# Differential scores as rounded high/low products in place of a float32 product with a block-diagonal key

## The chip, the core and the metric

The kernel runs on one core of a Trainium2 chip. The metric is the device time of one execution in microseconds; lower is better. The engines that matter here are TensorE (PE: matrix products; PEld is its weight load), VectorE (DVE), ScalarE (ACT), GpSimd (POOL) and SyncE (SP, whose queue starts the loads). Each works through its own list of instructions in order and waits for the others by semaphores.

## The reference

Two transformer blocks on 256 tokens of width 1024: latent attention, a convolutional FFN, differential attention, a second FFN and a hybrid layer. The change lies in the differential attention. Each of 8 heads has two maps j of 64 dimensions; each map has scores with a distance penalty and a softmax of its own, and the second map is taken off the first:

```python
qkv = x @ w_qkv
q = qkv[..., :2 * H * d].reshape(b, s, H, 2, d)        # H = 8, d = 64
k = qkv[..., 2 * H * d:4 * H * d].reshape(b, s, H, 2, d)
v = qkv[..., 4 * H * d:].reshape(b, s, H, 2 * d)
sc = jnp.einsum('bqhjd,bkhjd->bhjqk', qb, k) * scale
sc = sc - slopes[None, :, None, None, None] * dist[None, None, None]
p = jax.nn.softmax(sc, -1)
a = p[:, :, 0] - lam * p[:, :, 1]
o = jnp.einsum('bhqk,bkhd->bqhd', a, v)
o = rms_norm(o, subln_g) * (1.0 - lam_init)
return o.reshape(b, s, H * 2 * d) @ w_o
```

## The kernel before

Products with weights are done in three rounded products (`mm3`, L131 to L133): both operands are split into a high part, rounded to the type float32r, and a low part, the rest; high times high, high times low and low times high are added. A weight chunk of 128x1024 comes into a raw buffer, ScalarE makes its high part (`wload`, L116) and VectorE its low part (L117).

The differential layer (`diff`) first makes v for all heads. Then it goes through the heads. For each, `wload` brings the weights of q and k, and 48 products of 256 columns give q and k of the head, transposed (128 dimensions on partitions, 256 tokens), in one bank `mm` of PSUM; there are two such banks. The first map holds partitions 0 to 63, the second 64 to 127. ScalarE copies q (L689) into `dq` and the first map's k (L691) into the block-diagonal key `kbd`; VectorE copies the second map's k (L692). `kbd` is 128 x (2 x 256), zero off its two blocks, so that one product of 512 columns gives the scores of both maps (L699), in plain float32, for each of two blocks of 128 query tokens. The distance penalty is added by a bfloat16 product into the same bank (L700).

There is one score bank `s` (the last block of the last head takes an `mm` bank). Behind the scores comes, for each block, `softmax_rows`: the maximum over keys (L379) and its scaling (L380) on VectorE, two exponentials with their sums on ScalarE (L383), the reciprocal of the sums (L385) on VectorE. Then VectorE scales by lambda (L703), scales the first map (L704) and adds the second (L705). TensorE transposes the result (L707), ScalarE copies it to `aT` (L708), and TensorE multiplies by v (L711). After heads 3 and 7 the four heads are normed: squares on ScalarE (L719), sums (L720), eleven small operations and the scaling (L725) on VectorE, transposes on TensorE (L173), and the split into high and low parts (L127 on ScalarE, L128 on VectorE). The product with w_o (`wide`) starts with the key tiles of heads 0 to 3 and ends with those of heads 4 to 7. `boundary` then begins the next norm; its first products on TensorE are those at L275.

A scheduler sets the order on every engine when the program is built: it takes the operations of the whole program and moves independent ones ahead, so that projections of the next heads, and later products with w_o, stand between the scores of one head. A change of a few operations can therefore move rows on all engines.

Of the kernel before, what the change touches and what calls it, by code (L numbers as in the profile page):

```python
# [9 lines left out]
F32 = mybir.dt.float32  # L10
# [27 lines left out]
def build(tc, a, out):  # L38
# [15 lines left out]
    def banks(c2, **tags):  # L54
        """four banks of a layer, by tag; the other four are accumulators"""
        assert sum(tags.values()) == 4
        uid[0] += 1
        psx[0] = c2.enter_context(tc.tile_pool(name=f"ps{uid[0]}", bufs=1, space=bass.MemoryType.PSUM, reuse_waits="tile"))
        psx[1] = tags
# [40 lines left out]
    tsl = [slice(0, P), slice(P, 2 * P)]  # L100

    def wload(src, n, part=1024, tag="w", hb=HB, pool=None, eng=None, mk=None, scale=None):
        """a weight chunk [128, n]; returns its parts as (high, low) float32r tiles"""
# [36 lines left out]
    def rsqrt(v, n, mul=1.0):  # L140
        """v [P, n] (all positive) -> mul/sqrt(v): bit guess, one tuned and one cubic step."""
# [21 lines left out]
        # y1 is -1/K1 of the first step's value  # L163
# [4 lines left out]
    def tposes(src_list, dst_hi, dst_lo=None, scale=None, eng="v", tag="sm"):  # L168
        """transpose [P,128] pieces into one bank, then move to dst ([P, n, 128] view)."""
# [17 lines left out]
    def behind(*ins):  # L187
        """what is traced here goes behind these instructions on their engines"""
# [13 lines left out]
    def newton(ss, n, width, ins=False, mid=None):  # L202
        """1/sqrt(mean(x^2)+eps) from the scaled sums of one or two parts: bit guess and two Newton
        steps, the first with tuned constants; the sums come scaled so that no factor is left over."""
# [27 lines left out]
    def postnorm(pool, tb, bnk, g_bc):  # L232
        """h += rmsnorm(y) g"""
# [13 lines left out]
    def postnorm_cut(pool, tb, cut, g_bc):  # L247
        """the same for the last token block, in pieces that go out as they are done"""
# [15 lines left out]
    def prenorm(tb, g_bc, aft, warm_):  # L264
        """xT = transpose(rmsnorm(h) g) as high and low parts; 1/rms enters through the transposing product"""
        ss = small(2, F32, "ss2")
        # without a gain here it is in the weights that follow
        hg = [xp.tile([P, 512], F32, tag=f"hg{tb}{f}", name=nm("hg"), bufs=1) if g_bc is not None else h[:, tb, hf[f]] for f in range(2)]
        for f in range(2):
            j_ = square(h[:, tb, hf[f]], D, ss, f)  # L270
            if warm_:
                # keeps the clock of the tensor engine up while it waits
                b_ = smb()
                for _ in range(3):
                    nc.tensor.matmul(b_, j_[:, :P], j_, start=True, stop=True)  # L275
# [31 lines left out]
    def boundary(accs, post, pre):  # L307
        """residual add of one sublayer and the norm of the next, a token block at a time;
        returns xT and what is left to do of it, by token block"""
# [34 lines left out]
    def wide(src4, xT, bnk, mk=None, eng=None, hold=(), k0=4, cut=False):  # L344
        """generator: bnk[tb][f] = x @ w, w [1024, 1024] in four chunks of two k tiles; a step is one k tile
        of one token block, the first block's before the second's"""
# [28 lines left out]
    # ================= layer 0: MLA =================  # L375
    def softmax_rows(e, s_ps, n_tb, scale, width=S):
        """s_ps [P, n, w] psum -> e = exp(scale*(s-max)), returns 1/sum [P, n]"""
# [10 lines left out]
    def mla(xT, fin):  # L388
        with ExitStack() as c2:
# [10 lines left out]
            # the first two k tiles as plain float32 products  # L400
# [57 lines left out]
            def v_of(tb):                         # tokens on partitions  # L458
# [9 lines left out]
            def qr_of(tb):                        # rope part of q  # L468
# [93 lines left out]
    # ================= conv FFN =================  # L562
    def ffn(li, xT, fin, pre):
        with ExitStack() as c2:
# [6 lines left out]
            # the first two column tiles as plain float32 products, each token block as it comes  # L571
# [67 lines left out]
    # ================= layer 1: differential attention =================  # L639
    def diff(xT, fin):  # L640
        with ExitStack() as c2:
# [13 lines left out]
            kbd = [lp.tile([P, 2, S], F32, tag=f"kbd{i}", name=f"kbd{i}") for i in range(2)]  # L655
            for t in kbd:
                nc.gpsimd.memset(t, 0.0)
            # v
# [23 lines left out]
            for hd in range(H):  # L682
# [5 lines left out]
                q = lp.tile([P, S], F32, tag="dq", name=nm("dq"), bufs=2)  # L688
                nc.scalar.copy(q, b[:, 0])  # L689
                kb = kbd[hd % 2]  # L690
                nc.scalar.copy(kb[0:64, 0], b[0:64, 1])  # L691
                nc.vector.tensor_copy(kb[64:128, 1], b[64:128, 1])  # L692
# [4 lines left out]
                for tb in range(2):  # L697
                    sb = (mmb() if hd == H - 1 and tb else bank("s")).rearrange("p (t s) -> p t s", t=2)
                    nc.tensor.matmul(sb, q[:, tsl[tb]], kb, start=True, stop=False)  # L699
                    nc.tensor.matmul(sb, sid[:, hd], distb[:, tb:tb + 1, :].to_broadcast([P, 2, S]), start=False, stop=True)  # L700
# [31 lines left out]
    # ================= hybrid layer =================  # L732
    def hybrid(xT, fin):
        with ExitStack() as c2:
# [48 lines left out]
            oball = Vik                           # o takes the place of v, tokens on partitions  # L783
# [63 lines left out]
            QK = lt("QK", [P, H, 2, S])   # [:, :, 0] = k', [:, :, 1] = q'  (both doubled)  # L847
# [65 lines left out]
            # M[i,j] = -(k_i.k_j) e^(G_i-G_j) c_j for j < i, stored with j on partitions (A) and with i on partitions (M)  # L913
# [47 lines left out]
            # (I - M)^-1 of the 16 x 16 diagonal blocks by substitution, one block on a partition  # L961
# [44 lines left out]
            # blocks of 16 -> 32 -> 64 -> 128; a pair's off-diagonal block lies in the even rows and odd columns  # L1006
# [36 lines left out]
            # outputs, four heads at a time  # L1043
# [44 lines left out]
            def zproj(br, hp):  # L1088
                """(1 + tanh(z/2)) z = 2 silu(z) of two heads"""
# [238 lines left out]
```

## Time and profile before

| what | value |
|---|---|
| median of three runs | 1039.8 us (1038.62 to 1041.2) |
| the profiled execution: span from first to last instruction | 1037.8 us |
| PE busy | 1012.7 us (98%) |
| DVE busy | 738.0 us (71%) |
| ACT busy | 545.3 us (53%) |
| POOL busy | 33.1 us (3%) |
| share of TensorE in the chain that ended last | 84% |

The page gives no other time for the profiled execution than its span. Matrix products are pipelined and their ends modelled, so one product's duration overlaps the next; what a product costs in a stream is the step from its start to the start of the next one. The same holds for VectorE and ScalarE, where a row can start a little before the one ahead has ended. The granted TensorE clock is full through the stretches of this layer.

### The profile page before, as it was taken

The page shows a single profiled execution, that of the slowest core. Times are in us where ns is not written, and L with a number is a line of the kernel's source. Part 1 is how long each engine was busy: PE and PEld are TensorE (multiplying, and loading weights), DVE is VectorE, ACT ScalarE, POOL GpSimd, SP SyncE. Part 2 cuts the span into 40 slices and gives each one's busy share as a digit, 9 for nine tenths or more (in the row PEclk, how much of TensorE's full clock was granted, in tenths as well). Part 3 has the DMA queues.
Part 4 walks back from the last instruction along what each step waited for, and adds up shares of the span by engine and source line. Part 5 has one row for each costly group of instructions (what it writes and reads, how often), then busy time and mean ns, then how long its engine had stood idle before and what let it go on. Part 6 is the DMA issues. An engine that isn't in the chain of part 4 may idle for free.

```text
span 1037.8 us, 18147 instructions
## 1 busy us (share of the span) xinstructions
PE 1012.7 (98%) x7120; PEld 924.6 (89%) x7120; DVE 738.0 (71%) x1387; ACT 545.3 (53%) x949; POOL 33.1 (3%) x35
## 2 busy tenths in 40 slices
PE   8889899999999999999999999999999999999997
PEld 6778799999987888799999998799898999999996
DVE  5775687777668479778777767578799657685563
ACT  5653466555436456557555554465554455544451
POOL 0000100000012000010000001000203000000000
PEclk9999999999999999999999999999999999999999
DMA  7562467555325425276655442444244413455541
GB/s 276 173 219 81 168 204 222 186 185 179 124 93 189 158 100 172 88 243 234 205 185 187 156 141 76 162 162 164 81 135 102 141 54 113 160 181 185 183 163 41
DMA packets 55301, 162.70 MB, mean 157 GB/s; under 512 B 12784, under 2 KB 15280, under 8 KB 55216
## 3 DMA queue, kind: packets, MB, share of 16 engines
q1 hardware_dynamic: 55216, 161.55, 47.4%
q8 instruction: 56, 0.92, 0.3%
q14 instruction: 29, 0.24, 0.1%
HBM read 160.08 MB, written 1.44 MB: 156 GB/s over the span
## 4 chain that ended last, share of the span: by engine, by line
PE 84%; DVE 9%; ACT 3%; DMA 2%; issue 1%; SPq 0%; POOL 0%; DVEq 0%; ACTq 0%; POOLq 0%
PE mm L131 11%; PE mm L132 11%; PE mm L133 11%; PE acc L132 8%; PE acc L131 8%; PE acc L133 8%; PE sm L133 4%; PE sm L132 4%; PE sm L131 4%; PE mm L583 2%; PE acc L1019 2%; DVE lo L117 1%; PE acc L1054 1%; PE s L699 1%; ACT junk L199 1%
## 5 line engine op out<-in xcount | busy, mean ns | idle before, releaser
L117 DVE TENSOR_TENSOR lo<-raw,hi 128x1024 fp32r<-128x1024 f32 (+1 forms) x271 | 326.5, 1208 | 140.6 <-ACT hi L116 139.4
L116 ACT CAST hi<-raw 128x1024 fp32r<-128x1024 f32 (+1 forms) x271 | 278.2, 1035 | 244.6 <-PE mm L132 126.6
L133 PE MATMUL mm<-xT,lo 128*128 128x256 f32 x928 | 265.6, 286 | 0.0
L131 PE MATMUL mm<-xT,hi 128*128 128x256 f32 x928 | 265.3, 286 | 0.0
L132 PE MATMUL mm<-xT,hi 128*128 128x256 f32 x928 | 264.9, 285 | 0.0
L132 PEld LDWEIGHTS mm<-xT,hi 128*128 128x128 f32 x928 | 177.6, 191 | 1.9 <-issue 0.7
L131 PEld LDWEIGHTS mm<-xT,hi 128*128 128x128 f32 x928 | 177.5, 191 | 1.5 <-issue 0.3
L133 PEld LDWEIGHTS mm<-xT,lo 128*128 128x128 f32 x928 | 177.6, 191 | 1.3 <-issue 0.7
L131 PE MATMUL sm<-xT,hi 128*128 128x256 f32 (+1 forms) x328 | 92.8, 283 | 0.0
L133 PE MATMUL sm<-xT,lo 128*128 128x256 f32 (+1 forms) x328 | 92.8, 283 | 0.0
L132 PE MATMUL sm<-xT,hi 128*128 128x256 f32 (+1 forms) x328 | 92.8, 283 | 0.0
L131 PE MATMUL acc<-hi,gv 128*128 128x512 f32 x176 | 69.2, 393 | 0.0
L132 PE MATMUL acc<-lo,gv 128*128 128x512 f32 x176 | 69.0, 392 | 0.0
L133 PE MATMUL acc<-hi,gv 128*128 128x512 f32 x176 | 68.5, 389 | 0.0
L132 PEld LDWEIGHTS sm<-xT,hi 128*128 128x128 f32 (+1 forms) x328 | 62.2, 190 | 0.9
L131 PEld LDWEIGHTS sm<-xT,hi 128*128 128x128 f32 (+1 forms) x328 | 62.2, 190 | 0.8
L133 PEld LDWEIGHTS sm<-xT,lo 128*128 128x128 f32 (+1 forms) x328 | 62.2, 190 | 0.1
L383 ACT ACTIVATE e<-s,s 128x256 f32<-128x256 f32 x46 | 21.5, 472 | 34.6 <-DVE s L380 32.8
L133 PEld LDWEIGHTS acc<-hi,gv 128*128 128x128 f32 x176 | 33.1, 188 | 7.5 <-DVE gv L125 0.3
L131 PEld LDWEIGHTS acc<-hi,gv 128*128 128x128 f32 x176 | 33.2, 189 | 6.3 <-ACT gv L125 0.6
L132 PEld LDWEIGHTS acc<-lo,gv 128*128 128x128 f32 x176 | 33.2, 189 | 5.3
L131 PE MATMUL mm<-og,hi 128*128 128x256 f32 x128 | 36.0, 281 | 0.0
(462 smaller groups left out, 1905.0 us busy)
## 6 DMA issues: line engine op xcount, KB each, us to landing
raw<-in_ffn_up SPq DMA_DIRECT2D x88, 512.0 KB, 4.6
raw<-in_ffn_down SPq DMA_DIRECT2D x44, 512.0 KB, 4.4
raw<-in_diff_qk SPq DMA_DIRECT2D x16, 512.0 KB, 5.2
raw<-in_h_kq SPq DMA_DIRECT2D x16, 512.0 KB, 4.5
raw<-in_h_qk SPq DMA_DIRECT2D x16, 512.0 KB, 3.9
raw<-in_h_z SPq DMA_DIRECT2D x16, 512.0 KB, 3.7
raw<-in_h_gate SPq DMA_DIRECT2D x16, 512.0 KB, 4.5
raw<-in_h_br SPq DMA_DIRECT2D x16, 512.0 KB, 4.6
```

The source lines that it names most:

```text
L116: nc.scalar.copy(hi[:, :k], raw[:, :k])
L117: (eng or nc.vector).tensor_tensor(lo[:, :k], raw[:, :k], hi.bitcast(F32)[:, :k], op=ALU.subtract)
L131: nc.tensor.matmul(o, l[0], r[0], start=start, stop=False)
L132: nc.tensor.matmul(o, l[0], r[1], start=False, stop=False)
L133: return nc.tensor.matmul(o, l[1], r[0], start=False, stop=stop)
L199: nc.scalar.activation(junk[:, :p.shape[-1]], p, AF.Square, scale=math.sqrt(beta_of(width)), accum_out=ss[:, i:i + 1])
L383: nc.scalar.activation(e[:, i], s_ps[:, i], AF.Exp, bias=mx[:, i:i + 1], scale=scale, accum_out=sm[:, i:i + 1])
L583: last = nc.tensor.matmul(mmf[j][:, t, tsl[tb]], raws[j][t][:, kt * P:kt * P + P], xF[kt // 4][:, kt % 4, tsl[tb]], start=kt == 0, stop=kt ...
L699: nc.tensor.matmul(sb, q[:, tsl[tb]], kb, start=True, stop=False)
L1019: nc.tensor.matmul(b[:, i], lhs(i), rhs(i), start=True, stop=True)
L1054: nc.tensor.matmul(b[:, i], lhs(hds[i], i), rhs(hds[i], i), start=True, stop=True)
```

## The change

For each head q and k are no longer copied as float32. Per map m there is a tile `qk[m]` of 128 x (2 x 256) in float32r. ScalarE casts the map's 64 rows of q and k into the map's own half of the partitions (L694). The other half gets the low part of q, which VectorE makes by a subtraction (L696), and once more the high part of k, which ScalarE copies (L697). So one product over 128 partitions adds high times high and low times high. `klo` holds the low part of k in the map's half, a second subtraction on VectorE (L698), and zeros in the other; the product with it adds high times low. A block's scores become one distance product and four products of 256 columns in place of one float32 product of 512 columns and one distance product. The distance product comes first.

The core of the diff:

```diff
-            kbd = [lp.tile([P, 2, S], F32, tag=f"kbd{i}", name=f"kbd{i}") for i in range(2)]
-            for t in kbd:
-                nc.gpsimd.memset(t, 0.0)
+            klo = [lp.tile([P, 2, S], F32R, tag=f"klo{i}", name=f"klo{i}") for i in range(2)]
+            for t in klo:
+                nc.gpsimd.memset(t.bitcast(F32), 0.0)
...
-                q = lp.tile([P, S], F32, tag="dq", name=nm("dq"), bufs=2)
-                nc.scalar.copy(q, b[:, 0])
-                kb = kbd[hd % 2]
-                nc.scalar.copy(kb[0:64, 0], b[0:64, 1])
-                nc.vector.tensor_copy(kb[64:128, 1], b[64:128, 1])
+                b2 = [slice(0, 64), slice(64, P)]
+                qk = [lp.tile([P, 2, S], F32R, tag=f"qk{m}", name=nm("qk"), bufs=2) for m in range(2)]
+                kl = klo[hd % 2]
+                for m in range(2):
+                    nc.scalar.copy(qk[m][b2[m]], b[b2[m]])
+                for m in range(2):
+                    nc.vector.tensor_tensor(qk[m][b2[1 - m], 0], b[b2[m], 0], qk[m].bitcast(F32)[b2[m], 0], op=ALU.subtract)
+                    nc.scalar.copy(qk[m][b2[1 - m], 1], qk[m].bitcast(F32)[b2[m], 1])
+                    nc.vector.tensor_tensor(kl[b2[m], m], b[b2[m], 1], qk[m].bitcast(F32)[b2[m], 1], op=ALU.subtract)
...
-                    nc.tensor.matmul(sb, q[:, tsl[tb]], kb, start=True, stop=False)
-                    nc.tensor.matmul(sb, sid[:, hd], distb[:, tb:tb + 1, :].to_broadcast([P, 2, S]), start=False, stop=True)
+                    nc.tensor.matmul(sb, sid[:, hd], distb[:, tb:tb + 1, :].to_broadcast([P, 2, S]), start=True, stop=False)
+                    for m in range(2):
+                        nc.tensor.matmul(sb[:, m], qk[m][:, 0, tsl[tb]], qk[m][:, 1], start=False, stop=False)
+                        nc.tensor.matmul(sb[:, m], qk[m][:, 0, tsl[tb]], kl[:, m], start=False, stop=m == 1)
```

Lines behind the change move down by eight: L703 to L705 become L711 to L713, L720 becomes L728, L725 becomes L733. Some comments and docstrings go as well, which changes nothing.

Outside this layer no engine's order changes. Inside it, three places. On TensorE, the scores of head 2's first block, before:

```order
L132 MATMUL mm_3969<-xT_3314,hi_3959 128x256
L699 MATMUL s_3918<-kbd_3418,dq_3912 128x512
L707 MATMUL sm_3811<-c_ident,e_3832 128x128 x2
L700 LDWEIGHTS sid
L700 MATMUL s_3918<-distb,sid 128x512
L133 MATMUL mm_3969<-xT_3313,lo_3960 128x256
```

and now (mm is a projection bank, hi and lo are weights, sid and distb the slope and the distances):

```order
L131 MATMUL mm_4005<-xT_3313,hi_3995 128x256
L705 LDWEIGHTS sid
L705 MATMUL s_3948<-distb,sid 128x512
L707 MATMUL s_3948<-qk_3936 128x256
L708 MATMUL s_3948<-klo_3418,qk_3936 128x256
L707 MATMUL s_3948<-qk_3937 128x256
L132 MATMUL mm_4005<-xT_3314,hi_3995 128x256
L708 MATMUL s_3948<-klo_3418,qk_3937 128x256
```

One row has become four, the distance product stands ahead of them, and a projection product fills in before the last.

On VectorE, head 1's second block and the preparation of head 2 before (s are the small columns of maxima and sums, e the softmax rows):

```order
L379 TENSOR_REDUCE s_3833<-s_3829 128x2
L380 TENSOR_SCALAR s_3833<-s_3833 128x2
L385 RECIPROCAL s_3839<-s_3836 128x2
L703 TENSOR_TENSOR s_3839<-s_3839,nlam 128x1
L704 TENSOR_SCALAR e_3832<-e_3832,s_3839 128x256
L692 COPY kbd_3418<-mm_3863 64x256
L705 SCALAR_TENSOR_TENSOR e_3832<-e_3832,s_3839 128x256
L117 TENSOR_TENSOR lo_4215<-raw_4212,hi_4214 128x1024
```

and now:

```order
L379 TENSOR_REDUCE s_3857<-s_3850 128x2
L117 TENSOR_TENSOR lo_4275<-raw_4272,hi_4274 128x1024
L380 TENSOR_SCALAR s_3857<-s_3857 128x2
L696 TENSOR_TENSOR qk_3936<-mm_3887,qk_3936 64x256
L698 TENSOR_TENSOR klo_3418<-mm_3887,qk_3936 64x256
L696 TENSOR_TENSOR qk_3937<-mm_3887,qk_3937 64x256
L385 RECIPROCAL s_3863<-s_3860 128x2
L698 TENSOR_TENSOR klo_3418<-mm_3887,qk_3937 64x256
L711 TENSOR_TENSOR s_3863<-s_3863,nlam 128x1
L712 TENSOR_SCALAR e_3856<-e_3856,s_3863 128x256
```

Three of the four subtractions stand between the scaling of the maximum and the reciprocal, where nothing stood before.

On VectorE, the end of the second group norm before (on is the normed output, doT its split transpose, lo the weights of the FFN behind):

```order
L725 TENSOR_TENSOR on_4553<-acc_4169,s_4543 128x512
L725 TENSOR_TENSOR on_4562<-acc_4170,s_4543 128x512
L117 TENSOR_TENSOR lo_4994<-raw_4991,hi_4993 128x1024
L128 SCALAR_TENSOR_TENSOR doT_3636<-sm_4555,sg,doT_3635 128x4x128
L117 TENSOR_TENSOR lo_5000<-raw_4997,hi_4999 128x1024
L117 TENSOR_TENSOR lo_5088<-raw_5085,hi_5087 128x1024
```

and now:

```order
L733 TENSOR_TENSOR on_4649<-acc_4223,s_4639 128x512
L733 TENSOR_TENSOR on_4658<-acc_4224,s_4639 128x512
L117 TENSOR_TENSOR lo_5090<-raw_5087,hi_5089 128x1024
L117 TENSOR_TENSOR lo_5096<-raw_5093,hi_5095 128x1024
L128 SCALAR_TENSOR_TENSOR doT_3636<-sm_4651,sg,doT_3635 128x4x128
L117 TENSOR_TENSOR lo_5184<-raw_5181,hi_5183 128x1024
```

A second low part of weights has moved ahead of the first low part of the normed heads.

## Rows read from the trace of the kernel before

**Rows 1.** Stretches A, B, C: length; busy us of PE, PEld, DVE, ACT, POOL.

```profile
348.50:387.41 38.91, 38.88 (x260) 31.45 (x259) 26.53 (x62) 21.08 (x54) 0.00 (x0) 1.00 0.32 109
387.41:423.87 36.46, 35.83 (x223) 28.06 (x221) 30.83 (x77) 21.43 (x53) 0.00 (x0) 1.00 0.43 145
423.87:443.96 20.09, 19.94 (x94) 15.57 (x93) 16.28 (x35) 10.91 (x18) 1.03 (x1) 1.00 0.48 152
```

**Rows 2.** Timeline, PE, a score product: start us, duration us, engine, line, operation.

```profile
403.83 0.28 PE L132 MATMUL mm<-xT,hi 128*128 128x256 f32 x1
403.95 1.04 PE L699 MATMUL s<-kbd,dq 128*128 128x512 f32 x2
404.83 0.38 PE L700 MATMUL s<-distb,sid 128*128 128x512 bf16 x1
...
405.17 0.28 PE L131 MATMUL mm<-xT,hi 128*128 128x256 f32 x1
```

**Rows 3.** Waits of DVE in A and B: us in total, times, longest.

```profile
DVE s L385 <- ACT e L383: 10.9, 11, 1.1
DVE s L379 <- PE s L700: 3.1, 5, 1.4
```

**Rows 4.** Timeline, DVE, rows in a stream (columns as in rows 2).

```profile
404.06 0.16 DVE L385 RECIPROCAL s<-s 128x2 f32<-128x2 f32 x1
404.26 0.16 DVE L703 TENSOR_TENSOR s<-s,nlam 128x1 f32<-128x1 f32 x1
404.34 0.34 DVE L704 TENSOR_SCALAR e<-e,s 128x256 f32<-128x256 f32 x1
404.71 0.43 DVE L692 COPY kbd<-mm 64x256 f32<-64x256 f32 x1
405.17 0.48 DVE L705 SCALAR_TENSOR_TENSOR e<-e,s 128x256 f32<-128x256 f32 x1
405.69 0.69 DVE L379 TENSOR_REDUCE s<-s 128x2 f32<-128x512 f32 x1
406.30 1.22 DVE L117 TENSOR_TENSOR lo<-raw,hi 128x1024 fp32r<-128x1024 f32 x1
407.43 0.16 DVE L380 TENSOR_SCALAR s<-s 128x2 f32<-128x2 f32 x1
```

**Rows 5.** Timeline, DVE, two rows that follow each other without L692.

```profile
400.35 0.48 DVE L705 SCALAR_TENSOR_TENSOR e<-e,s 128x256 f32<-128x256 f32 x1
400.75 0.69 DVE L379 TENSOR_REDUCE s<-s 128x2 f32<-128x512 f32 x1
```

**Rows 6.** Groups by line and shape: busy us, mean ns; idle before and releaser.

```profile
L125 DVE TENSOR_TENSOR oT<-o,oT 128x256 fp32r<-128x256 f32 x8 | 3.4, 419 | 3.5 <-ACT oT L125 3.5
...
L689 ACT COPY dq<-mm 128x256 f32<-128x256 f32 x8 | 3.0, 370 | 0.1
L708 ACT COPY aT<-sm 128x512 f32<-128x512 f32 x8 | 4.7, 587 | 7.7 <-PE sm L707 7.7
```

**Rows 7.** Timeline, DVE: starts of A and B, an unfilled reciprocal, B's last row.

```profile
348.50 0.43 DVE L692 COPY kbd<-mm 64x256 f32<-64x256 f32 x1
...
387.41 1.28 DVE L720 TENSOR_REDUCE s<-dsq 128x4 f32<-128x512 f32 x2 [0.27 <-ACT dsq L719]
...
416.45 0.17 DVE L380 TENSOR_SCALAR s<-s 128x2 f32<-128x2 f32 x1
417.77 0.17 DVE L385 RECIPROCAL s<-s 128x2 f32<-128x2 f32 x1 [1.15 <-ACT e L383]
...
423.39 0.48 DVE L705 SCALAR_TENSOR_TENSOR e<-e,s 128x256 f32<-128x256 f32 x1
```

**Rows 8.** Timeline, DVE, the second group norm's end in C.

```profile
430.03 1.29 DVE L725 TENSOR_TENSOR on<-acc,s 128x512 f32<-128x512 f32 x2
...
432.37 0.74 DVE L128 SCALAR_TENSOR_TENSOR doT<-sm,sg,doT 128x512 fp32r<-128x512 f32 x1
```

**Rows 9.** Timeline, PE, the end of C.

```profile
443.96 0.82 PE L275 MATMUL sm<-junk 128*128 128x512 bf16 x3
```

## Prediction

> **What bounds the kernel now.** I read the windows first, cut at three landmarks of the differential layer. Stretch A runs from the first copy of a head into its block-diagonal key (L692) to the group norm of heads 0 to 3 (L720), B from there to the end of the last head's last softmax row (L705), C from there to the products at L275 that open the next norm [rows 1, 7]. In A and B together TensorE is busy 74.71 of 75.37 us: it always finds another projection to run, so today it is the bound. But VectorE is second: 26.53 of 38.91 us in A (68%) and 30.83 of 36.46 in B (85%). ScalarE has 42.5 of 75.37.
>
> The PE timeline next, for the price of a score product. The float32 product takes two passes: the first starts at 403.95, the distance product L700 at 404.83 (0.88), and the second projection product behind it at 405.17. From 403.95 to 405.17 are 1.22 us; less one projection product of 0.12 (403.83 to 403.95) the pair L699 + L700 takes 1.10, of which L700 is 0.22 [rows 2].
>
> Then VectorE's waits: its longest is at the reciprocal L385, 10.9 us in 11 times, because the two exponentials on ScalarE stand between it and the scaled maximum [rows 3]. That loop is short of fillers and nothing in the change shortens it.
>
> **TensorE's part: a gain of 6.4 us, if it stays the bound.** Each of 16 float32 products (eight heads, two token blocks) becomes four high/low products of 256 columns. That is the shape of the projection products, 0.12 each, with weight loads that their stream already hides. So 1.10 becomes 0.22 + 4 x 0.12 = 0.70, 0.40 less, 16 times: 6.4 us.
>
> **VectorE's part: 11.0 us more.** One copy per head (L692) becomes four subtractions (L696 and L698, twice each). Price: L692 starts at 404.71 and the next row at 405.17, so 0.46 [rows 4]. The new rows read PSUM and write 64 partitions x 256, as L692 does; the subtraction of that length and type in the trace, the low part of oT at L125, lasts 0.419 [rows 6], and L692 0.43. So 0.46 is the nearest, the upper end. The lower end is 0.34: where two ordinary rows follow each other the second starts before the first has ended (L705 at 400.35 lasts 0.48, L379 starts at 400.75, 0.08 early) [rows 5], and 0.42 - 0.08 = 0.34. L692 shows no such overlap on either side (404.34 + 0.34, then 404.71; 404.71 + 0.43, then 405.17), nor does the L379 that next reads PSUM (405.17 + 0.48, then 405.69). All new rows change the partition half they read or write, so I take 0.46: 32 x 0.46 = 14.7 us for 8 x 0.46 = 3.7.
>
> [...]
>
> The whole VectorE queue of A and B, row by row, at start-to-start prices [rows 4, 5, 7, 8]:
> - one softmax block: L379 0.61, L380 0.20 (0.17 and a gap), L385 0.20, L703 0.08, L704 0.37, L705 0.40, together 1.86; 16 blocks 29.8
> - 17 low parts of weights (L117) at 1.13 (406.30 to 407.43): 19.2
> - the norm of heads 0 to 3: two L720 1.28, eleven small rows at 0.20, two L725 1.29, two L128 1.48: 6.2
> - the key copies: 3.7 before, 14.7 after.
>
> That is 58.9 before, in 75.37 us, so VectorE idles 16.5. After it is 69.9. The order of the changed kernel has the same 17 L117 there and one softmax block more in A (nine, then seven).
>
> How much idle remains? An unfilled reciprocal costs 417.77 - 416.45 - 0.20 = 1.12 [rows 7]. In the new order I looked at every block for what stands between its L380 and its L385. At ten of 16 there are new subtractions, an L117, rows of the norm or of another block, enough to cover the exponentials but for one case below; at six nothing stands there (head 0 block 0, head 2 block 1, head 3 block 0, head 6 both, head 7 block 0). They can't be helped: with one score bank the next block's scores wait for the same exponentials. 6 x 1.12 = 6.7. To these I add 1.1, my estimate by following the queues: 0.65 at head 4 block 0, where the copy of aT stands between its two exponentials on ScalarE, and 0.5 at head 2 block 1, whose scores come late. So 7.8 us. A and B: 69.9 + 7.8 = 77.7, against 75.37: **2.3 us longer**. By stretch A gets 20 subtractions, nine L117, nine blocks and 4.5 of waits (40.6, 1.7 longer), B the rest (37.1, 0.6 longer). TensorE's own work there falls to 68.3, so it waits over 9 us.
>
> **Stretch C.** L705 to the last norm's L725 is the same chain as before. Behind it, before, one L117 stands ahead of the L128 that gives the first low part of the normed heads; now two do. L725 starts at 430.03 and L128 at 432.37 [rows 8]; the second L117 puts L128 1.13 later, and TensorE has used up its products of heads 0 to 3 by then. The rest to L275 (443.96) [rows 9] is products back to back. **1.1 us longer**; nothing, if the weights of that L117 come late and it isn't in the way.
>
> **Edits taken at nothing.** ScalarE gets two casts of 64x512 and two of 64x256 for two copies: 2 x 0.587 + 2 x 0.37 for 2 x 0.37 [rows 6], about 1.2 more per head, 9.4 in all; with 42.5 busy of 75.37 this lies beside VectorE's queue. Uncovered, where an exponential queues behind them, it costs up to 1.2 at a head. A projection bank is now held until the fourth subtraction, about 1.4 longer; there are two, and a projection alone takes 48 x 0.12 = 5.8. On the SP queue two gains go behind six weight loads, and on POOL one norm product ahead of a cast; both are needed much later. The first distance product moves ahead into the value projection: 0.2, within the rounding.
>
> **Sum.** 2.3 + 1.1 = 3.4 us. The profiled execution has a span of 1037.8, 2.0 under the median of 1039.8; the span goes to 1041.2 and the time to 1043.2. A measurement can tell 0.3%, 3.1 us, from no change.
>
> **The rivals.**
> 1. *TensorE stays the bound* (faster, the other side): the subtractions fill waits and A and B shrink by 6.4, less about 1 for new waits: 5.4, so 1034.4. For this VectorE must get through in 70.0 us: less 6.7 of waits nothing fills and 55.2 of other work, 8.1 are left for 32 subtractions, 0.25 each. The lower bound is 0.34 and L704, a plain SBUF row, starts its successor after 0.37. Chance 0.14.
> 2. *The two engines come out even*: the subtractions overlap after all (0.34, so 32 x 0.12 = 3.8 off), or the L117 in C isn't in the way, or both. With both, A and B take 73.9, 1.5 less: 1038.3; with only C away, 1042.1. Middle 1040.5, chance 0.33. [...]
> 3. *The waits don't fill*: the queue is at 90%, each late subtraction delays scores, and these the next maximum. Idle then stays nearer the 16.5 of before, say 12: A and B 81.9, 6.5 longer, and C 1.1: 1047.4. Ten blocks have something to fill with, so chance 0.12.
> 4. *Forecast*: VectorE is the bound, 1041.8 to 1045.5, middle 1043.2. Chance 0.41.
>
> **How the numbers follow.** Faster by over 0.3%: rival 1 and a little of 2, 0.16. Slower by over 0.3%: rival 3 and nearly all of the forecast from 1042.9 up, 0.50; the rest, 0.34, is within. For eight in ten the range reaches from 1036.5, which leaves out most of rival 1, to 1047.0. The forecast stands close to the 0.3% line; its own range is 1041.8 to 1045.5.
>
> **What would show it.** L696 and L698 starting 0.45 to 0.48 after each other; VectorE busy over 67 us between its first subtraction and the last softmax row; that stretch near 77.7; TensorE's idle there 9 us instead of 0.7, ended mostly by VectorE; the first L128 of the last norm behind two L117. Wrong it would be if the subtractions overlap, if TensorE still has no idle time in that stretch (rival 1), or if the waits at L385 stay at 10 us (rival 3).

## The result, and the profile after

The changed kernel is slower: 1046.8 us (median of 6 runs) against 1039.2 (6 runs), ratio 1.0077 with an interval of 1.0057 to 1.0097, so 7.6 us where 3.4 were forecast. The profiled execution, the fastest of the six (1044.2), has a span of 1042.1.

The windows of the changed kernel, stretches A, B and C (length; busy us and rows of PE, PEld, DVE, ACT, POOL; granted clock; DMA share; GB/s), cut at the same landmarks as [rows 1]:

```profile
345.71:387.15 41.44, 40.84 (x314) 38.13 (x313) 34.86 (x83) 28.55 (x69) 0.00 (x0) 1.00 0.37 117
387.15:424.69 37.54, 33.40 (x216) 28.48 (x216) 31.39 (x80) 23.67 (x54) 0.00 (x0) 0.95 0.38 125
424.69:446.73 22.04, 17.95 (x78) 13.56 (x77) 16.29 (x35) 10.48 (x18) 1.03 (x1) 0.92 0.45 149
```

A is 2.5 us longer than in [rows 1], B 1.1 and C 2.0: 101.0 for 95.5, or 5.6 us. The new column to look at is the third from the right. It was 1.00 in all three stretches; now it is 0.95 in B and 0.92 in C. (The spans differ by 4.3 only: A starts at 348.5 in the trace of before and at 345.7 here, and over all traces of kernels that are alike up to there its start lies between 345.7 and 349.9.)

The new rows themselves, and the wait at the reciprocal, in the groups by line and shape of VectorE in A and B (L696 and L698 are the subtractions; busy us, mean ns, idle before and its releaser):

```profile
L696 DVE TENSOR_TENSOR qk<-mm,qk 64x256 fp32r<-64x256 f32 x16 | 6.7, 422 | 0.7 <-ACT qk L694 0.2
L698 DVE TENSOR_TENSOR klo<-mm,qk 64x256 fp32r<-64x256 f32 x16 | 6.7, 420 | 0.4
...
L385 DVE RECIPROCAL s<-s 128x2 f32<-128x2 f32 x16 | 2.6, 163 | 7.6 <-ACT e L383 7.5
```

Prices and waits are close to those of the prediction: a row lasts 0.42 and its successor starts 0.45 later in the mean, where 0.46 was counted, and the waits at L385 are 7.5 us where 6.7 and 0.65 were. (The prediction took 0.46 for each of the 32 rows, as if none overlapped the row ahead. In the trace 28 start behind the end of the row ahead; four, each behind a row that is no subtraction, start 0.08 to 0.10 us before it.) What the prediction did not have is in TensorE's timeline. First in B, at the fifth head's transposes (L715), then in C, at those of the last group norm (L173):

```profile
402.04 0.66 PE L173 MATMUL sm<-c_ident,on 128*128 128x128 f32 x4 [0.45 <-DVE doT L128]
404.96 0.66 PE L715 MATMUL sm<-c_ident,e 128*128 128x128 f32 x4 [2.27 <-DVE doT L128]
406.53 2.07 PE L719 MATMUL acc<-v,aT 128*128 128x128 f32 x8 [0.91 <-ACT aT L716]
...
428.17 0.40 PE L133 MATMUL mm<-hi,doT 128*128 128x512 f32 x1
431.75 0.66 PE L173 MATMUL sm<-c_ident,on 128*128 128x128 f32 x4 [3.18 <-DVE on L733]
433.21 0.67 PE L131 MATMUL acc<-hi,doT 128*128 128x512 f32 x1 [0.80 <-ACT doT L127]
433.68 0.63 PE L132 MATMUL acc<-lo,doT 128*128 128x512 f32 x1
434.10 0.63 PE L131 MATMUL acc<-hi,doT 128*128 128x512 f32 x1
```

The brackets are the waits: 2.27 us, in which the one transposing bank `sm` is full until VectorE's L128 has emptied it, and 3.18 us, in which TensorE has nothing left but the last norm. Behind each the steps are long: the products at 433.68 and 434.10 are 0.42 apart where such a pair was 0.23 apart before:

```profile
432.55 0.40 PE L132 MATMUL acc<-lo,doT 128*128 128x512 f32 x1
432.78 0.40 PE L131 MATMUL acc<-hi,doT 128*128 128x512 f32 x1
```

The windows of the changed kernel around the two waits say why (same columns as for A, B and C):

```profile
400.00:405.00 5.00, 2.28 (x18) 1.71 (x16) 4.97 (x6) 2.75 (x4) 0.00 (x0) 1.00 0.42 127
405.00:408.00 3.00, 2.09 (x11) 1.85 (x12) 2.93 (x6) 1.51 (x5) 0.00 (x0) 0.68 0.76 246
408.00:411.00 3.00, 3.00 (x16) 2.56 (x15) 1.20 (x3) 1.47 (x3) 0.00 (x0) 0.76 0.94 354
...
428.00:432.00 4.00, 0.82 (x5) 0.38 (x4) 3.52 (x15) 4.00 (x5) 0.00 (x0) 1.00 0.00 0
432.00:436.00 4.00, 3.08 (x12) 1.94 (x11) 4.00 (x5) 1.15 (x2) 0.00 (x0) 0.67 0.36 95
436.00:440.00 4.00, 4.00 (x18) 3.27 (x17) 3.28 (x4) 0.69 (x1) 0.00 (x0) 0.90 0.85 274
```

TensorE is idle for half of 400 to 405 and most of 428 to 432. In these two windows its granted clock is still 1.00; in those that follow it is 0.68 and 0.76 behind the first wait, 0.67 and 0.90 behind the second. That the waits are the cause this trace alone doesn't show.

So the theory to test (D): VectorE's rows set A and B as forecast, and the waits that they make cost a second time, through the clock. Rivals: the new products are dear in themselves (P); the order in which TensorE's work was laid out is at fault (O); the clock falls with the execution, not with this layer (X).

### The profile page after: what moved, and what is told of

It reads as the page before. It is cut to its first block, busy times and chain, and to the rows that moved or that the text cites. A ratio compares the mean times of both kernels' runs of the same rounds, so it can differ in the third digit from the quotient of the medians.

```text
span 1042.1 us, 18243 instructions
## 1 busy us (share of the span) xinstructions
PE 1011.0 (97%) x7152; PEld 930.2 (89%) x7152; DVE 747.0 (72%) x1411; ACT 555.2 (53%) x965; POOL 33.9 (3%) x35
## 4 chain that ended last, share of the span: by engine, by line
PE 80%; DVE 12%; ACT 3%; issue 2%; DMA 2%; SPq 0%; POOL 0%; DVEq 0%; ACTq 0%; POOLq 0%
PE mm L131 11%; PE mm L132 11%; PE mm L133 11%; PE acc L132 7%; PE acc L131 7%; PE acc L133 7%; PE sm L133 4%; PE sm L132 4%; PE sm L131 4%; DVE lo L117 3%; PE mm L583 2%; PE acc L1027 2%; PE acc L1062 1%; ACT junk L199 1%; PE sm L290 1%
## 5 line engine op out<-in xcount | busy, mean ns | idle before, releaser
L117 DVE TENSOR_TENSOR lo<-raw,hi 128x1024 fp32r<-128x1024 f32 (+1 forms) x271 | 326.5, 1209 | 135.4 <-ACT hi L116 134.0
```

Source lines behind the costliest of these rows:

```text
L117: (eng or nc.vector).tensor_tensor(lo[:, :k], raw[:, :k], hi.bitcast(F32)[:, :k], op=ALU.subtract)
```

## Experiments

Line numbers shift by a few from kernel to kernel. "Before" is always the run of the same session, and times are medians. Each time is followed by its ratio to before, with the 95% interval in brackets. Edits are shown shortened, partly in words. Where the recorded texts of the first runs say "the sixth head's" transposes, the fifth head's are meant, those at L715 above.

**The changed kernel again.** No edit.

> The changed kernel once more, for a second trace of it. Theory D: the granted clock falls again behind TensorE's waits at the sixth head's transposes and at the last group norm (0.6 to 0.8 and 0.6 to 0.9 for some 4 to 6 us each), stretches A, B, C again near 41.5, 37.5 and 22.0 us. Rival X (the drops come with the execution and not with these waits): in this trace they lie elsewhere, and stretches B and C are 1 to 2 us shorter or longer. Time 1045 to 1048 in both.

1048.05 against 1040.78, 1.0064 (1.0039 to 1.0089). A, B, C: 41.46, 38.34, 22.99, granted clock 1.00, 0.91, 0.85. The falls are at the same two waits, and longer: 0.62 and 0.50 in the windows 405 to 408 and 408 to 411, 0.63 and 0.52 in 432 to 436 and 436 to 440. X falls for these two.

**The two halves of the change, each alone.** Products without rows:

```
-  subtract q (both maps), subtract k (both maps)
+  subtract q (first map only); the other low parts stay zero
```

> The changed kernel with one subtraction per head on VectorE instead of four (the low part of the keys and the low part of the second map's queries are left out, so this part of the computation is missing); all new float32r products and all casts stay. Theory D (the added VectorE rows make TensorE wait, and the waits lower its granted clock): with 24 rows of 0.42 us gone VectorE's queue is as long as before and TensorE is bound again, now with 6.4 us less work in stretches A and B, so they take 69 to 73 us instead of 79.0, granted clock 1.00 there, no TensorE wait over 1 us before the sixth head's products, and the time is 5 to 9 us under the changed kernel's: 1037 to 1042. Rival P (the new products themselves, with twice the weight loads and the mm bank held through the casts, cost more than the float32 ones): stretches A and B stay at 77 to 79 us and the time at 1044 to 1048. Rival X (the clock drops elsewhere in the program and the layer has little to do with it): layer shorter but the time within 2 us of the changed kernel's.

Rows without products: the float32 products of before, with the casts and three subtractions per head added to its one copy.

> The kernel before with its float32 score products, plus the four casts and three of the subtractions per head of the change, whose results nobody reads. Theory D: VectorE's queue is the changed kernel's, so stretches A and B take 77 to 79 us although TensorE has 6.4 us more work to do in them; TensorE waits less than in the changed kernel, its clock may fall less; time 1043 to 1047. Rival P (the products cost the time): 1039 to 1041, since VectorE's rows hide under TensorE as the half-idle VectorE of before would allow; stretches A and B within 1 us of 75.4.

Products alone: 1040.91 against 1040.78, 1.0004 (0.9982 to 1.0026). Rows alone: 1050.57, 1.0101 (1.0062 to 1.0139). Their windows, products alone first:

```profile
347.57:386.94 39.37, 39.26 (x302) 36.27 (x301) 27.80 (x64) 27.59 (x65) 0.00 (x0) 1.00 0.38 121
386.94:421.15 34.21, 33.55 (x231) 29.44 (x230) 28.27 (x74) 24.39 (x58) 0.00 (x0) 1.00 0.42 139
421.15:444.37 23.22, 18.78 (x76) 14.17 (x75) 16.30 (x35) 10.48 (x18) 1.03 (x1) 0.85 0.41 139
```

```profile
346.58:390.99 44.41, 44.19 (x293) 35.73 (x292) 34.67 (x79) 27.77 (x65) 0.00 (x0) 1.00 0.32 108
390.99:428.07 37.08, 36.15 (x213) 27.85 (x211) 32.42 (x85) 23.95 (x58) 0.00 (x0) 1.00 0.39 129
428.07:450.22 22.15, 17.03 (x72) 13.21 (x72) 16.30 (x35) 10.58 (x18) 1.03 (x1) 0.85 0.43 146
```

The loss comes with VectorE's rows and not with the new products: 24 rows off the changed kernel give back its 7 us, and 24 rows added to the kernel before, together with the casts, cost 8.2 us in the layer. P falls. The second run isn't the clean test of VectorE's queue that it was meant to be, though. Its time lies above D's range (1043 to 1047) and A and B, with 81.49, above the 77 to 79; TensorE is busy 80.34 us there, for the order gives it 23 rows more than before (x506 for x483) and C 22 fewer, so that it idles in C, 4.3 us in one wait, at 0.85 of the clock.

For the products alone D has the time, but it had not foreseen that they gain nothing. A and B fall only from 75.4 to 73.6 (69 to 73 were expected), and C gives that back: TensorE runs dry (x76 rows there for x94 in [rows 1]), waits 3.64 us, and the clock falls to 0.85.

**Is it the order?** In both kernels with new products TensorE's order has the output products of heads 0 to 3 ahead of the last head's end. Here 24 of them are held behind it:

```
   run(wide(a["diff_o"], oT, bs, mk=ring(lp)
+      , products of token block 1 behind the last L719 of head 7
```

> The kernel with the new products and one subtraction per head (low parts of the keys and of the second map's queries left out, as in the run of the products alone), and with the second token block's output products of heads 0 to 3 (24, 0.23 us each) held behind the last head's products. That run had TensorE wait 3.64 us in C and the same time as before. Theory O (its order spent these products too early, and C's chain took the gain back): A and B shrink from 73.6 to 69 to 71, C falls from 23.2 to 20 to 21.3 at granted clock 1.00, time 4 to 6 us under the kernel before, 1034 to 1037. Rival (the chain of softmax blocks bounds A and B, so TensorE waits there instead): A and B 72 to 73.6, now with waits, time 1037 to 1040.

> The changed kernel with the same 24 output products held behind the last head's. VectorE's queue stays as long. Theory D with the clock as a term: C falls from 22 to 23 to 20.2 to 21.3, since TensorE has 5 us of work for the wait ahead of the last norm's transposes, but B loses these products as fillers and keeps its length (37.5 to 38.5) or gets slower through a lower clock; time 1044 to 1047. Rival O (order alone is what costs): A, B and C together fall to 96 or less, time under 1042.

With the products alone: 1040.63 against 1039.28, 1.0013 (0.9997 to 1.0029). With the changed kernel: 1047.64, 1.0084 (1.0061 to 1.0106). Both as without the hold. Windows of A, B and C with the products alone and held, then what VectorE waited for in A and B:

```profile
348.67:388.05 39.38, 39.25 (x302) 36.26 (x301) 27.80 (x64) 27.60 (x65) 0.00 (x0) 1.00 0.37 121
388.05:422.28 34.23, 30.68 (x216) 26.95 (x214) 28.28 (x74) 24.39 (x58) 0.00 (x0) 1.00 0.43 139
422.28:443.71 21.43, 20.70 (x90) 16.56 (x91) 16.49 (x35) 11.02 (x18) 1.03 (x1) 0.92 0.42 141
```

```profile
DVE s L386 <- ACT e L384: 9.0, 8, 1.6
DVE s L380 <- PE s L713: 4.9, 6, 0.9
```

A and B are not a hundredth shorter in sum (73.61 for 73.58), though TensorE now idles 3.55 us in B. So what bounds B there is not TensorE but the chain of softmax blocks: the exponentials between VectorE's rows and the scores that come after them (9.0 and 4.9 us of waits in A and B). For A this isn't shown: TensorE is busy 39.25 of 39.38 us there, the hold leaves its order in A as it was, and VectorE waits 3.6 us for its scores, so another order might gain something in A. As the kernels are, TensorE's 6.4 us were worth 1.8 in A and B. And holding the products only moves the wait from C to the end of B: with the changed kernel C has 0.87 of the clock, B 0.94, and the three stretches 101.25. O falls for these 24 products; no other change of the order was tried.

**ScalarE's part.** The copies of the keys to the other half (L697) are left out, with the changed kernel and with the products alone.

> The changed kernel without ScalarE's copies of the keys' high part to the other half of the array (L697, 16 of 0.40 us; the tiles hold zeros there, so the product of the queries' low part is left out); VectorE's rows and TensorE's products all stay. If ScalarE's added casts lie beside VectorE's queue, as the prediction took them (at nothing): A and B within 0.7 us of 79.0, time within 1.5 us of the changed kernel's, 1045 to 1048. Rival (ScalarE's casts stand ahead of the exponentials and lengthen the chain of softmax blocks): A and B shrink by 2 to 4 us, time 1042 to 1044.

> The new products with one subtraction per head and without the copies L697 (left out: all but the high parts' product and, for one map, nothing more), so that VectorE's and ScalarE's queues are close to those of the kernel before. With the copies this kernel took as long as the kernel before, with A and B at 73.6 and C at 23.2. If ScalarE's casts took the products' gain: A and B fall to 69 to 71.5. If the chain of VectorE's and ScalarE's softmax rows alone, which before has too, bounds A and B as soon as TensorE gets 2 us faster: A and B stay at 72.5 to 74, C at 22 to 23.5 with a wait of 3 to 4 us and a lowered clock behind it, time within 2 us of the kernel before.

The first gave 1051.26 against 1039.54, 1.0125 (1.0096 to 1.0154), and 82.1 us in A and B: slower with less work. The order on the engines changed with the edit, TensorE waited 3.3 us for L128 in B where it had waited 2.27, and the run tells nothing on ScalarE. The second gave 1039.53 against 1039.54, 1.0000 (0.9977 to 1.0024), A and B 72.23, C 23.34 at 0.85 of the clock: without the 16 copies A and B are 1.35 us shorter, between the two expectations. The order on the engines changed here too, so the 1.35 can't be put down to the copies alone.

**The clock.** Filler products that nobody reads keep TensorE busy in a wait. In C alone:

```
   r = rsqrt(ss, 8)
+  last head: 3 x nc.tensor.matmul(sm bank, sq[:, 0], sq)
```

> The changed kernel with three float32 products into the scores' bank, which nobody reads, ahead of the last group norm's transposes (TensorE waited 3.18 us there, and its granted clock was 0.67 and 0.90 in the 8 us behind). Theory D with the clock as a term of its own: stretch C falls from 22.0 to 20.3 to 21 us, the granted clock there is 1.00, and the time is 1.0 to 1.7 us lower, 1045 to 1046. Rival (VectorE's two L117 ahead of the transposes' evictions set stretch C whatever the clock does): C stays within 0.4 us of 22.0, the time 1046 to 1048, for then the products only fill a wait.

1046.46 against 1040.78, 1.0060 (1.0038 to 1.0081). C is 21.37 at clock 1.00 (22.04 and 22.99 without). The time moved by less than its uncertainty; the stretch decides, and no other row of the layer changed its place. In B I first tried to take the cause of the wait away, by giving the first norm's transposes a projection bank:

> The changed kernel with the three filler products ahead of the last norm's transposes, and with the first norm's transposes in one of the two projection banks instead of the scores' transposing bank, so that the fifth head's transposes (TensorE waited 2.27 us there, and its granted clock fell to 0.68 and 0.76 behind) don't wait for the first norm's evictions. If the missing part of the forecast is the clock: granted clock 1.00 in A to C, A and B 77.5 to 78.3, C 21.2 to 21.4, together 3.3 to 4.2 us over the kernel before, time 1042.5 to 1044.5. Rival (VectorE's queue is simply longer than counted): the wait moves to another place, A and B stay at 79 or more and the time at 1045 to 1047.

1057.94 against 1039.28, 1.0173 (1.0136 to 1.0209): a failure. With one of the two projection banks given to the norm the order left 100 of TensorE's rows out of A (x214 for x314), and it was busy only 32.00 of 39.41 us there. The run says nothing on the clock. So fillers went into B's wait as well, three behind the first norm's last transposes, into the accumulator of heads 4 to 7. Ahead of them every row kept its place; behind them three rows of TensorE and one each of VectorE and ScalarE moved by a few places:

> The changed kernel with three float32 filler products (0.88 us each, read by nobody) ahead of the fifth head's transposes, where TensorE waited 2.27 us for the first norm's evictions, and three more ahead of the last norm's transposes, as in the run with fillers in C alone. Every other row stays in its place. Theory D with the clock as a term: granted clock 1.00 in A, B and C; A stays at 41.4, B falls from 37.5 to 38.3 to 36.2 to 36.9, C to 21.4; together 99.0 to 99.8, 3.5 to 4.3 us more than before, which is the forecast's 3.4 within 1; time 1042.5 to 1044.5. Rival (B is set by the queues of VectorE and ScalarE and the clock there costs nothing): clock 1.00 but B at 37.5 or more, time 1045 to 1047.

> The changed kernel with fillers in both waits once more, for a second trace. If the forecast plus the clock holds: A 41.4, B 36.3 to 36.6, C 21.4, granted clock 1.00 in all three, time 3.4 to 4.5 us over the kernel before. Open besides: at 796 to 804 us, far behind this layer, the clock fell to 0.5 to 0.8 in both profiles of the changed kernel, behind a TensorE wait of 1.8 us that the kernel before has too, and not in the first trace of this one. If that comes with the execution and not with this layer, it may be here as well, 1 to 3 us longer behind the layer.

1043.59 against 1039.54, 1.0039 (1.0021 to 1.0058), and 1043.16 against 1039.05, 1.0048 (1.0025 to 1.0072): 4.1 us slower than before, twice. Windows of the first:

```profile
347.71:389.13 41.42, 40.84 (x314) 38.12 (x313) 34.84 (x83) 28.56 (x69) 0.00 (x0) 1.00 0.37 117
389.13:425.55 36.42, 34.34 (x222) 28.28 (x222) 31.49 (x80) 23.77 (x54) 0.00 (x0) 1.00 0.40 129
425.55:446.92 21.37, 19.12 (x84) 13.62 (x84) 16.29 (x35) 10.53 (x18) 1.04 (x1) 1.00 0.47 155
```

A is as it was; B is 36.42 instead of 37.54 and 38.34, C 21.37 instead of 22.04 and 22.99, with more work on TensorE than before the edit. The second trace has 41.45, 36.38 and 21.38.

Where in B the gain arises can be read row by row. Up to 20.7 us into B each of VectorE's rows starts within 0.07 us of the same time with and without fillers. The next row is the maximum over the scores that TensorE makes behind the wait, first in the changed kernel, then with fillers:

```profile
409.79 0.69 DVE L379 TENSOR_REDUCE s<-s 128x2 f32<-128x512 f32 x1 [1.57 <-PE s L708]
```

```profile
410.55 0.69 DVE L380 TENSOR_REDUCE s<-s 128x2 f32<-128x512 f32 x1 [0.27 <-PE s L713]
```

From the start of B that is 22.64 and 21.42 us, and 1.1 of this 1.2 stays to the end of B. That is the clock, priced: 1.8 and 3.6 us of the layer in the two traces of the changed kernel. The executions without a trace agree. The granted clock, as a mean over the whole program, has a median of 0.990 in 12 executions of the changed kernel, 0.993 in eight with fillers in C, and 0.997 in 17 with fillers in both waits; the kernel before has 0.996 to 0.998, session by session.

**Relief for VectorE.** Low parts of every other head's weights (L117) on GpSimd:

> The changed kernel with the low parts (L117) of every other head's query and key weights computed on GpSimd instead of VectorE: 8 of the 17 in stretches A and B, 8 x 1.13 = 9 us, leave VectorE's queue. Theory D (VectorE's queue sets A and B): they shrink from 79.0 by most of what TensorE waits there, to 71 to 75, the wait at the fifth head's transposes behind the first norm's L128 falls from 2.27 to under 1 us, the granted clock in B is 1.00, time 1038 to 1042. Rival O (the order on TensorE, in which the output products of heads 0 to 3 come ahead of the last head's work and leave stretch C without any, takes the gain back): A and B shrink, but C grows or stays at 22 to 23, with TensorE waiting over 3 us ahead of the last norm's transposes; time 1041 to 1045. Rival G (GpSimd, 1.54 us for 512 columns at L279, so some 3 us for each low part, delivers the weights late): A and B at 79 or more, TensorE waiting for L117, time 1047 or more.

1051.53 against 1039.28, 1.0109 (1.0070 to 1.0148): worse than the changed kernel, on the side of G, with 47.22 us in A, but not for the weights alone. Timeline of VectorE, and of GpSimd beside it:

```profile
364.05 1.75 DVE L380 TENSOR_SCALAR s<-s 128x2 f32<-128x2 f32 x1
```

```profile
363.39 2.39 POOL L117 TENSOR_TENSOR lo<-raw,hi 128x1024 fp32r<-128x1024 f32 x1 [11.98 <-ACT hi L116]
```

L380, a row of 0.17 us, takes 1.75 and ends 0.02 after GpSimd's row. In A its nine have a mean of 691 ns and those of L711 309 instead of 158, together 6.1 us more, as much as the five L117 that left VectorE there. So the run is no clean test of VectorE's queue. Why these rows are so long beside GpSimd's it doesn't show. Relief that puts nothing on GpSimd: the scaling of the first map on ScalarE, complete as the changed kernel is.

```
-  nc.vector.tensor_scalar(e[:, 0], e[:, 0], rs[:, 0:1], None, op0=ALU.mult)
+  nc.scalar.activation(e[:, 0], e[:, 0], AF.Identity, scale=rs[:, 0:1])
```

> The changed kernel with the scaling of the first map's exponentials (L712, 16 rows of 0.35 us on VectorE) on ScalarE; nothing is left out. VectorE's queue in A and B gets 16 x 0.37 = 5.9 us shorter, each softmax block's chain gets a hand-over to ScalarE and back. If the length of VectorE's queue sets A and B: they shrink by 2 to 5 us, time 1041 to 1045. Rival (the chain from a block's scores to its transposes counts, not the queue): A and B are unchanged or up to 4 us longer, time 1046 to 1051.

1044.17 against 1039.54, 1.0055 (1.0034 to 1.0075). VectorE is busy 61.78 us in A and B for 66.25, and they last 74.14 for 78.98 (77.84 with a full clock, above): 3.7 us for 4.5, as it must be if its queue sets them. (The order on the engines moved here too.) But C is 22.94, since TensorE now waits 4.57 us there and gets 0.85 of its clock. With fillers in that wait, and likewise for the products alone:

> The changed kernel, complete, with the scaling of the first map on ScalarE (that run had A 39.4, B 34.7, C 22.9 with granted clock 0.85 behind a wait of 4.57 us) and with five filler products in that wait. If the clock is what C loses there: C 20.2 to 21.4 at granted clock 1.00, A, B and C together 94.3 to 95.5 against 95.5 before, time 1038 to 1041, so all that the change lost is back but nothing is won. Rival (C is held by its chain, or the fillers are in the way): C 22.5 or more, time 1042 to 1045.

> The new products with one subtraction per head (low parts of the keys and of the second map's queries left out), which alone took as long as the kernel before, now with four float32 filler products (0.88 us each, read by nobody) in TensorE's 3.64 us wait ahead of the last norm's transposes. If the clock behind that wait took the products' gain: A and B stay at 73.6, C falls from 23.2 to 20.2 to 21.4 at granted clock 1.00, together 93.8 to 95, 0.5 to 1.7 us less than before, time 0.5 to 3 us under the kernel before. Rival (C is held by the chain of the norm, whatever the clock): C at 22.5 or more, time equal to the kernel before. In both, most of the 6.4 us that TensorE no longer needs stays lost, as idle time or filler.

ScalarE's scaling with fillers: 1039.79 against 1039.05, 1.0008 (0.9990 to 1.0026); the windows:

```profile
346.34:385.74 39.40, 38.80 (x303) 36.54 (x302) 31.50 (x70) 30.82 (x73) 0.00 (x0) 1.00 0.39 121
385.74:420.48 34.74, 34.23 (x234) 30.04 (x233) 30.30 (x77) 28.14 (x66) 0.00 (x0) 1.00 0.42 137
420.48:441.86 21.38, 19.69 (x83) 13.40 (x82) 16.31 (x34) 10.58 (x18) 1.03 (x1) 1.00 0.46 154
```

95.52 for the 95.46 of before: all that the change lost is back and nothing is won. Products alone with fillers: 1039.42, 1.0013 (0.9988 to 1.0037); A, B, C 39.36, 34.23, 21.37, or 94.96. The stretches are as expected, the time isn't (0.5 to 3 us under before): half a us is too little for it to show.

With fillers in its wait C is 21.37 or 21.38 at full clock in five traces of five, whatever stands ahead of it. (The run with a projection bank given to the norm has 22.04 at full clock, in another order.) So C is a chain of its own, 1.3 longer than in the kernel before. VectorE and then TensorE in C, changed kernel with fillers in both waits:

```profile
433.10 2.35 DVE L117 TENSOR_TENSOR lo<-raw,hi 128x1024 fp32r<-128x1024 f32 x2
435.37 0.74 DVE L128 SCALAR_TENSOR_TENSOR doT<-sm,sg,doT 128x512 fp32r<-128x512 f32 x1
```

```profile
436.17 0.66 PE L173 MATMUL sm<-c_ident,on 128*128 128x128 f32 x4 [0.84 <-DVE doT L128]
```

From the start of C to the first L128 are 9.82 us, where before it was 8.50 [rows 8]; from there to L275 11.55 and 11.59. So the whole 1.3 lies ahead of L128, where the second L117 stands, and TensorE's next transposes wait 0.84 us for that L128 to empty the bank. No run took this L117 away, so it is a reading of the trace. I found no version that beats the kernel before.

## Why the prediction was right in its working and wrong in its sum

- **TensorE saves 6.4 us: right as work, worth 1.8.** Busy TensorE in the three stretches falls from 94.65 to 88.8 for the products alone (92.34 less four fillers of 0.88, [rows 2]), so 5.8. But with 24 of the 32 rows off VectorE, A and B gained only 1.8; in B the chain of softmax blocks stood that close behind TensorE. Rival 1 (5.4 of gain) did not come near even so.
- **VectorE +11.0 us, A and B +2.3: right.** With the clock held up, A and B last 77.84 and 77.83; the forecast was 77.7. That it is so close is in part luck: A is 0.8 too long for it (41.4 for 40.6) and B 0.7 too short (36.4 for 37.1), and VectorE is busy 66.25 us there, not over 67. That a row costs 0.46 because it changes its partition half was the author's reading of L692, and no run shows it as the cause; what the trace shows is the mean step of 0.45, with four of the 32 rows overlapping the row ahead.
- **C +1.1: right.** 21.37 at full clock, 1.28 over [rows 1], all of it ahead of the first L128, as the prediction said.
- **The sum: the failed step.** The prediction wrote that TensorE "waits over 9 us" and has no term for what these waits do to TensorE itself: the sum is 2.3 + 1.1, all at full clock, and none of its rivals has the clock either. At full clock the layer costs 3.75 (99.21 for 95.46) and the time 4.1, against 3.4. The rest, 3.2 to 3.5 us of the medians (7.6 and 7.3 less 4.1), went with the fillers: in the layer the lower clock took 1.8 and 3.6 us in the two traces. (The medians alone don't split it, see what stays open.) So the layer's work was forecast well and its time wasn't: 1046.8 lies above the forecast's own 1041.8 to 1045.5, and that it is still within the wider range, up to 1047.0, is luck. The kernel had a hint: the products at L275, which the prediction used as the mark for the end of C, are fillers of this kind, six that nobody reads, from 443.96 to 445.65 in the trace of before, where TensorE's next product starts at 446.00 and the granted clock is 1.00 from 440 to 452. No run took them away, so what they do to the clock isn't shown. The lower clock comes from two waits that the prediction could have placed: the fifth head's transposes behind the one bank that VectorE empties late, and the last norm, for which C has no products left.
- **TensorE's idle was misplaced.** Its work in A and B did not fall to 68.3; at full clock it is 72.5 (75.18 in the fillers' trace, less three of 0.88), since products of C moved ahead. So the changed kernel's TensorE idles 4.7 us in A and B, not 9, and another 4.1 in C, where there is nothing left to fill with.
- **ScalarE's casts at nothing: open.** Without the copies A and B were 1.35 us shorter where VectorE isn't the bound, but in another order; where it is the bound, the run tells nothing.
- **Rival 3** (waits don't fill, 1047.4) has the number and not the mechanism: the waits at L385 are 7.5 us, as in the forecast.

What stays open: far behind this layer TensorE waits 1.8 us once more, in the kernel before too, and in both traces of the changed kernel the clock fell there (0.82 and 0.75 in the windows 796 to 800 and 800 to 804; 0.71, 0.50 and 0.51 from 800 to 812 in the second). The part behind the layer was 595.4 and 598.6 us long for 593.8. Of the 17 traces nine show such a fall and eight don't. Among the eight are the kernel before, the products alone, both traces with fillers in both waits, and the one with fillers in C alone, in which the clock still fell in B; among the nine are the products alone with fillers in C. So in these traces it goes neither with VectorE's rows nor with the fall in B, and what decides it is not known. A part of what the medians lost may be this; the windows of the layer, on which the sum above rests, don't contain it.

## What to carry over

When a change takes work off the bound, look for the next engine's chain before you count the gain: here 1.8 us were left of a saving of 6.4. When a change makes TensorE wait, count the wait, and then look at the clock behind it: here it was 0.68 and 0.67 in the windows behind two waits, and with fillers in both the layer was 1.8 us shorter (3.6 against the second trace). Fillers in the wait are a cheap way to tell the two apart. A stretch that ends a layer can have a chain of its own, as C has, and then work moved out of it leaves it no shorter.

## What was unexpected on the chip

- The same wait does not always lower the clock: TensorE waits 1.80 us at 795 in the kernel before and its clock stays at 1.00; 1.81 us at 797.88 in the changed kernel, and it is 0.75 from 800 to 804.
- Leaving 16 copies out made the kernel some 4 us slower than the changed one (1.0125 for 1.0064 and 1.0077). It has less work; what else changed is the order on the engines, with a longer wait in B (3.3 us for 2.27).
- A tiny row on VectorE (L380, 0.17 us) took 1.75 us beside a GpSimd row that it shares no data with.
